# Second group's scores of layer 0 moved into the mixer stage, two gate spans of eight blocks, one-hot tiles with token pairs innermost

## The chip, the cores and the metric

One core of one Trainium2 chip runs the kernel. The time is device microseconds of one execution on that core; every value of the kernel is float32 unless a tile is marked F16. The profile names the engines PE (matrix products), PEld (their weight loads), DVE (vector), ACT (activation), POOL and SP.

## The reference

A step of a two-layer hybrid encoder, on 512 prompt rows (four blocks B0 to B3 of 128) and 64 sample rows (S), 1024 wide.

```
for each layer l in (0, 1):
    x += concat(DiffAttention, mLSTM, ChunkMLP)(rmsnorm(x) @ w_in) @ w_out     # the mixer
    q = rmsnorm(x) @ peer_wq                # 8 heads, two halves of 128 each
    s1, s2 = q_half @ keys.T                # 128 scores each; top 16 of each half
    e = top 16 of the 16 x 16 sums          # expert number: key1 * 128 + key2
    g = softmax of the 16 chosen sums       # per head
    h = gelu(u[e] . xn) * g                 # 8 x 16 = 128 experts a token, of 16384
    x += sum over e of h * v[e]             # the PEER step
y = rmsnorm(x)
```

The mixer's attention of a prompt block looks at its own and the earlier blocks, so B2 and B3 need B0 and B1 of the same layer, and not the other way round.

## The kernel before, in words

The tokens are in two groups, g1 = B0, B1, S and g2 = B2, B3. In each layer the groups pass a mixer stage and a PEER step. The mixer stage is made of parts: N (norm and transposes), P and Q (projections), M (mix), O (out projection), S (PEER queries, key scores and their top-16 selection, `scores` and `select_heads`), F (`finish_select`: expert numbers, softmax, and for dense blocks the transposed key numbers and gates in the tile `sel`). `ORDER` (L55) is the order of the parts by layer, written by hand; parts joined by "+" are woven, one step of each in turn (`weave`, L93). Each engine takes its instructions in an order that the scheduler builds at compile time from priorities, which are the program order; what `low` (L997) issues gets 10 million added and yields to everything else that is ready.

**PEER is done in two ways.** In each layer two blocks are dense: B0 and B1 in layer 0, B2 and B3 in layer 1. The others are sparse (S, B2, B3 in layer 0; S, B0, B1 in layer 1).

*Dense* (`peer_dense`, L1046): 128 chunks of 128 experts. `lead(c)` loads a U chunk (512 KB, queue of SP), does 8 matmuls into one half of the tile H (L1057) and a gelu on ACT into a tile A (L1066). Then A is multiplied by a slice of a gate block W on DVE (L1090), a V chunk (512 KB) is loaded, and 8 matmuls add to y (L1097). Leads run ahead of y by `LAG[l]` chunks; A has `LAG[l]` + 2 slots, and the first 8 x `PRE[l]` activations lie in gate blocks instead.

*Gate blocks.* W[experts of 8 chunks, 256 tokens] exist for 16 groups of 8 chunks. `gate_batch` (L1008) fills 8 tokens of several blocks at once: DVE compares the token's second key with 0 to 127 (o2, L1015), the first key with the block's own numbers (o1, L1016), and multiplies o1 by the gate's two F16 parts (L1018). PE makes 16 matmuls per batch (L1022), ACT copies the result into W (L1024). A span of blocks needs 32 batches. `QB` (L40) gives the spans: 4, 4 and 8 blocks. The first span is made in `first_gate` (L1033), the later ones in the last `WIN` chunks of the span ahead (L1079 to L1085). The tiles o2 and o1 have the 8 tokens innermost, so a matmul of one token steps over 8 F16 values, 16 bytes. `HOME` says in which pool a block lies: 0, "a" (beside the stream buffers) or "b" (`wb2`, memory that the selection's pool `sp` has until `close_scores`, L172; o1 lies there too, and in layer 0's first span in a spare block, "hot").

*Sparse* (`gather_u`, `gather_v`, L964 and L985): for each of 128 expert slots (64 for S) POOL gathers 128 rows of U by index (512 KB, L953) and DVE reduces them against the norm (L977); then the same with V, added to x (L989). All of it is issued by `low`. In layer 0 the first of it is held behind the last DVE operation of the first gate (`self.gated`, L973). B3's V rows of layer 0 run in layer 1's mixer, woven with M1 (`rest_v`, part R).

**Order around the change.** Layer 0's mixer stage ends with "S1+M2 F1 O2". `run` (L1147 to L1154) then does the norm of B0 and B1 for the dense stage, weaves `first_gate` with 2 leads, weaves 8 further leads with the scores of g2, finishes the selection of g2, and only then calls `close_scores`. In layer 1 the scores of g2 run in the dense stage too, ahead of `first_gate`, beside 24 leads.

Of the kernel before, what the change touches and what calls it, by code (L numbers as in the profile page):

```python
# [21 lines left out]
P = 128  # L22
# [17 lines left out]
QB = [[4, 4, 8], [4, 4, 8]]  # L40
WIN = [[14, 24], [16, 16]]
GATE_A, GATE_B = 4, [6, 5]
HOME = ["0aaaabbbbbb0aaaa", "0aabbbbbaa0aabbb"]
# [6 lines left out]
LAG = [2, 8]  # L50
PRE = [0, 2]
EARLY_LEADS = 5
LATE_LEADS = 8
REST_STEP, REST_PARTS = 4, 16
ORDER = ["N1 P1 N2 Q1 M1+P2 O1+Q2 S1+M2 F1 O2", "N1 P1 Q1 M1+R O1 S1 N2 P2 F1+Q2 M2 O2"]  # L55
# [65 lines left out]
class Build:  # L121
# [30 lines left out]
    def dense_pools(self, ec, l):  # L152
# [13 lines left out]
        self.whp, self.mixer = None, False  # L166
        ec = self.sel_es.enter_context
# [70 lines left out]
    def setup(self):  # L238
# [13 lines left out]
        self.jj = self.cp.tile([P, P, 8], F16, name="jj")  # L252

    def make_bias(self):
# [3 lines left out]
        nc.vector.tensor_copy(self.jj, iota[:, :, None].to_broadcast([P, P, 8]))  # L258
# [585 lines left out]
    def finish_select(self, l, g):  # L844
        nc = self.nc
        for t in sorted(g, key=lambda t: t.order):
# [34 lines left out]
            c0, c1 = t.c0, t.c0 + P  # L881
            for j in range(2):
                nc.scalar.activation(self.sel[:, j, c0:c1], pt[:, j, :], AF.Copy)
            gr = self.sp.tile([P, P], F32, tag="gr", name="gr")
            nc.scalar.activation(gr, pt[:, 2, :], AF.Copy, scale=GSCALE)
            nc.vector.tensor_copy(self.sel[:, 2, c0:c1], gr)
            nc.vector.tensor_tensor(self.sel[:, 3, c0:c1], gr, self.sel[:, 2, c0:c1], op=ALU.subtract)
# [36 lines left out]
    def lookup(self, t, h0, nh):  # L924
# [14 lines left out]
        for a in range(2):  # L939
            oh = self.sp.tile([P, TOPK, 16, PH], F16, tag="oh", name="oh")[:, :, :, :nh]  # L940
            nc.vector.tensor_tensor(oh, self.jj[:, None, :16, :nh].to_broadcast(sh),
# [55 lines left out]
    def low(self, fn, *a):  # L997
        p0 = self.tc.cur_priority
        self.tc.cur_priority = p0 + LOW
        fn(*a)  # L1000
        self.tc.cur_priority = p0
# [6 lines left out]
    def gate_batch(self, blocks, i0, t0, pb, hot=None):  # L1008
        nc, nq = self.nc, 8 * len(blocks)
        if hot is None:  # L1010
            o2 = self.d2.tile([P, P, 8], F16, tag="o2", name="o2")
            o1 = self.wb2.tile([P, 3, 64, 8], F16, tag="o1", name="o1", bufs=2)[:, :, :nq, :]
        else:
            o2, o1 = hot
        nc.vector.tensor_tensor(o2, self.jj, self.sel[:, 1, None, t0:t0 + 8].to_broadcast([P, P, 8]), op=ALU.is_equal)  # L1015
        nc.vector.tensor_tensor(o1[:, 2], self.jj[:, i0:i0 + nq, :], self.sel[:, 0, None, t0:t0 + 8].to_broadcast([P, nq, 8]),  # L1016
                                op=ALU.is_equal)
        self.mark = nc.vector.tensor_tensor(o1[:, 0:2], o1[:, 2:3].to_broadcast([P, 2, nq, 8]),  # L1018
                                            self.sel[:, 2:4, None, t0:t0 + 8].to_broadcast([P, 2, nq, 8]), op=ALU.mult)
        for j in range(8):  # L1020
            for p in range(2):
                nc.tensor.matmul(pb[:, j, :nq], o2[:, :, j], o1[:, p, :, j], start=(p == 0), stop=(p == 1))  # L1022
# [242 lines left out]
```

## Time and profile before

| what | value |
|---|---|
| median of 3 runs | 3736.93 us (3736.39 to 3742.16) |
| profiled execution, its own time | 3738.22 us |
| its span | 3736.5 us |
| granted TensorE clock, mean | 0.929 |
| busy: PE, DVE, POOL, ACT | 87%, 70%, 41%, 18% |
| bytes moved | 1060.34 MB, mean 284 GB/s |

Two lines of the page show the course of the work, in 40 equal slices of 93 us; the digits are tenths busy.

```profile
PE   8989879938999999998986796567678999999998
...
DVE  4554777898766666656068999879998767666641
```

Counted from 1, layer 0's mixer stage lasts into slice 6, its dense stage into slice 19, layer 1's mixer stage into slice 31, and the rest is its dense stage. A digit of 9 says that PE is the engine to look at there; where PE falls and DVE rises (slices 9, 25 to 30) it is DVE.

### The profile page before, as it was taken

To read this page: it belongs to the slowest core of one execution; us is meant where nothing else is said; L and a number is where in the kernel's file an instruction comes from. 1 tells how busy PE (TensorE), PEld (TensorE's weight loads), DVE (VectorE), ACT (ScalarE), POOL (GpSimd) and SP (SyncE) were. 2 spreads that over 40 slices of the span, in tenths; PEclk is the share of its full clock that TensorE was granted. 3 is DMA by queue.
4 is the path that set the end of the run, shared out by engine and by line. 5 is a ranking of instruction groups with operands and counts; after the bars stand their busy time and mean duration, and the time that the engine had idled before them with its cause. 6 is when DMAs were issued, how large, how long until landed. Compare 5 with 4: busy or idle time off the path is not lost.

```text
span 3736.5 us, 43654 instructions
## 1 busy us (share of the span) xinstructions
PE 3244.7 (87%) x14408; PEld 2238.5 (60%) x14408; DVE 2598.5 (70%) x6106; ACT 690.3 (18%) x2591; POOL 1531.7 (41%) x1284
## 2 busy tenths in 40 slices
PE   8989879938999999998986796567678999999998
PEld 6767657726777555554453554345565667766655
DVE  4554777898766666656068999879998767666641
ACT  5444232102121000001221222211121102100000
POOL 0000004455434655555036534655664553454420
PEclk9999988969999999999988898678888999999999
DMA  5332327978978999999368887989898898899973
GB/s 181 98 104 72 105 82 299 372 261 311 323 250 293 390 378 396 387 379 354 100 183 317 323 301 270 292 309 349 323 321 286 324 401 278 313 410 409 409 277 123
DMA packets 299937, 1060.34 MB, mean 284 GB/s; under 512 B 36372, under 2 KB 39232, under 8 KB 299712
## 3 DMA queue, kind: packets, MB, share of 16 engines
q0 software_dynamic: 184320, 671.17, 49.9%
q1 hardware_dynamic: 115392, 386.38, 28.1%
q8 instruction: 115, 1.88, 0.2%
q14 instruction: 110, 0.90, 0.1%
HBM read 1048.09 MB, written 8.27 MB: 283 GB/s over the span
## 4 chain that ended last, share of the span: by engine, by line
PE 61%; DVE 17%; DMA 13%; issue 5%; ACT 2%; POOL 1%; another core or an unknown queue 0%; SPq 0%; DVEq 0%; ACTq 0%; POOLq 0%
PE y L1097 19%; PE H L1057 18%; DMA row<-in_peer_v_dram,idx 8%; PE ps L392 7%; PE ps L403 5%; PE ps L1022 5%; DVE row L977 4%; DMA row<-in_peer_u_dram,idx 2%; DVE x_b L989 2%; PE ps L214 1%; POOL row L953 1%; DVE x_s L989 1%; DMA V<-in_peer_v_dram 1%; PE ps L568 1%; PE ps L570 1%
## 5 line engine op out<-in xcount | busy, mean ns | idle before, releaser
L953 POOL DMA_INDIRECT row<-in_peer_u_dram,idx x640 | 772.9, 1208 | 1331.2 <-DVE row L977 616.9
L953 POOL DMA_INDIRECT row<-in_peer_v_dram,idx x640 | 758.5, 1185 | 729.8 <-DVE x_b L989 475.2
L1097 PE MATMUL y<-V,A 128*128 128x512 f32 x1920 | 872.8, 598 | 12.5 <-DMA V<-in_peer_v_dram 12.5
L977 DVE SCALAR_TENSOR_TENSOR row<-row,xn 128x1024 f32<-128x1024 f32 x640 | 768.0, 1221 | 80.6 <-DMA row<-in_peer_u_dram,idx 74.5
L989 DVE SCALAR_TENSOR_TENSOR x_b<-row,hb,x_b 128x1024 f32<-128x1024 f32 x512 | 656.2, 1282 | 119.4 <-DMA row<-in_peer_v_dram,idx 106.8
L1097 PEld LDWEIGHTS y<-V,A 128*128 128x128 f32 x1920 | 365.3, 192 | 376.1 <-issue 361.7
L1057 PE MATMUL H<-xTd,U 128*128 128x256 f32 x2048 | 480.8, 388 | 37.7 <-ACT A L1066 35.5
L1057 PE MATMUL H<-xT,U 128*128 128x256 f32 x2048 | 478.6, 387 | 39.5 <-ACT pre L1066 19.7
L1057 PEld LDWEIGHTS H<-xTd,U 128*128 128x128 f32 x2048 | 385.2, 192 | 155.7 <-ACT A L1066 97.6
L1057 PEld LDWEIGHTS H<-xT,U 128*128 128x128 f32 x2048 | 393.7, 194 | 131.7 <-issue 55.4
L1090 DVE TENSOR_TENSOR A<-A,W 128x256 f32<-128x256 f32 x240 | 101.1, 423 | 393.2 <-ACT A L1066 385.5
L403 PE MATMUL ps<-xT,w 128*128 128x320 f32 (+1 forms) x1280 | 339.3, 420 | 25.0 <-DMA w<-in_wt_dram 16.2
L1066 ACT ACTIVATE A<-H 128x256 f32<-128x256 f32 x240 | 92.0, 384 | 1360.2 <-PE y L1097 677.4
L1022 PE MATMUL ps<-o,o 128*128 128x32 f16 (+1 forms) x2560 | 237.5, 264 | 102.7 <-DVE o L1018 102.7
L1022 PEld LDWEIGHTS <-o 128*128 128x128 f16 x2560 | 228.5, 151 | 143.6 <-DVE o L1018 104.5
L403 PEld LDWEIGHTS ps<-xT,w 128*128 128x128 f32 x1280 | 246.5, 196 | 96.1 <-DMA w<-in_wt_dram 16.6
L1024 ACT ACTIVATE W<-ps 128x64 f32<-128x64 f32 x1024 | 154.5, 307 | 386.9 <-PE ps L1022 363.1
L1015 DVE TENSOR_TENSOR o<-jj,sel 128x1024 f16<-128x1024 f16 x160 | 110.3, 690 | 108.5 <-PE ps L1022 104.9
L989 DVE SCALAR_TENSOR_TENSOR x_s<-row,hb,x_s 128x1024 f32<-128x1024 f32 x128 | 164.2, 1283 | 15.6 <-DMA row<-in_peer_v_dram,idx 14.1
L392 PE MATMUL ps<-w,xT 128*128 128x512 f32 (+3 forms) x320 | 127.1, 548 | 3.5 <-DMA w<-in_wn_dram 3.4
L347 DVE TENSOR_TENSOR wl<-w,wh 128x1024 fp32r<-128x1024 f32 (+1 forms) x56 | 64.4, 1149 | 75.3 <-PE ps L392 55.3
L392 PE MATMUL ps<-w,mix 128*128 128x512 f32 (+1 forms) x224 | 110.9, 648 | 5.5 <-DMA w<-in_wn_dram 3.9
(318 smaller groups left out, 3065.3 us busy)
## 6 DMA issues: line engine op xcount, KB each, us to landing
V<-in_peer_v_dram SPq DMA_DIRECT2D x256, 512.0 KB
U<-in_uT_dram SPq DMA_DIRECT2D x256, 512.0 KB
w<-in_wt_dram SPq DMA_DIRECT2D x96, 512.0 KB
w<-in_wn_dram SPq DMA_DIRECT2D x80, 512.0 KB
row<-in_peer_u_dram,idx POOLq DMA_INDIRECT x640
row<-in_peer_v_dram,idx POOLq DMA_INDIRECT x640
w<-in_keysT_dram SPq DMA_DIRECT2D x16, 256.0 KB
w<-in_wn_dram SPq DMA_DIRECT2D x8, 264.0 KB
```

Source lines behind the costliest of these rows:

```text
L392: self.nc.tensor.matmul(p[:t.n, :wd], x[kk][:, t.c0:t.c0 + t.n], ww[:, k * wd:(k + 1) * wd], start=(kk + part + j == 0), stop=(kk == KC - ...
L403: self.nc.tensor.matmul(ps, ww[:, k * P:(k + 1) * P], x[k][:, :n], start=(k + part + j == 0), stop=(k == KC - 1 and part == pair and j == ...
L953: self.nc.gpsimd.indirect_dma_start(out=row, out_offset=None, in_=self.h[tab], in_offset=bass.IndirectOffsetOnAxis(ap=t.idx[:, k:k + 1], a ...
L977: nc.vector.scalar_tensor_tensor(row, row, 1.0, xn, op0=ALU.mult, op1=ALU.mult, accum_out=hb[:, k:k + 1])
L989: op = nc.vector.scalar_tensor_tensor(x, row, t.hb[:, k:k + 1], x, op0=ALU.mult, op1=ALU.add)
L1015: nc.vector.tensor_tensor(o2, self.jj, self.sel[:, 1, None, t0:t0 + 8].to_broadcast([P, P, 8]), op=ALU.is_equal)
L1022: nc.tensor.matmul(pb[:, j, :nq], o2[:, :, j], o1[:, p, :, j], start=(p == 0), stop=(p == 1))
L1024: nc.scalar.activation(W[:, :, t0:t0 + 8].rearrange("p i t -> p t i"), pb[:, :, 8 * i:8 * i + 8], AF.Copy, scale=1.0 / GSCALE)
L1057: mm = nc.tensor.matmul(hp, U[:, k, :], xT[k], start=(k == 0), stop=(k == KC - 1))
L1066: nc.scalar.activation(a, hp, AF.Gelu)
L1090: gated = nc.vector.tensor_tensor(a, a, Ws[ci // 8][:, ci % 8, :], op=ALU.mult)
L1097: nc.tensor.matmul(ys[i][:, hf, :], a[:, i * P:(i + 1) * P], V[:, hf * 512:(hf + 1) * 512], start=(c == 0), stop=(c == NCH - 1))
```

## The change

The scores of g2 in layer 0 become a part of the mixer stage (S2, the last of its order), and their finish follows with a priority of its own (MID, ahead of the gathers, behind the rest). `close_scores` is called at once when layer 0's dense pools are opened. Both layers have two gate spans of 8 blocks; the second is made in the last 24 (layer 0) or 16 (layer 1) chunks of the first. Layer 0 takes 12 leads ahead (LAG 4, PRE 1) instead of 2, then 8 beside the scores. The one-hot tiles, the number table `jj` and `sel` are laid out with pairs of tokens innermost, so a matmul of one token steps over 2 F16 values, 4 bytes; the lookup of expert numbers gets a table of its own, `jl`.

```diff
@@ -37,22 +37,22 @@
 WT = 1056
 TD = 256
 NG = TD + NS
-QB = [[4, 4, 8], [4, 4, 8]]
-WIN = [[14, 24], [16, 16]]
+QB = [[8, 8], [8, 8]]
+WIN = [[24], [16]]
 GATE_A, GATE_B = 4, [6, 5]
-HOME = ["0aaaabbbbbb0aaaa", "0aabbbbbaa0aabbb"]
+HOME = ["0aaabbbbbba0aaab", "0aabbbbbaa0aabbb"]
+MID = 10 ** 6
 LOW = 10 ** 7
 PS_TAG = {"p": "mm", "a": "mm", "r": "mm", "o": "o", "tp": "tr", "ta": "tr", "tr": "tr"}
 PS_BUFS = {"mm": 4, "tr": 3, "o": 1}
 T_TAG = {"p": "t", "a": "t", "r": "tr"}
 T_BUFS = {"t": 4, "tr": 2}
 DENSE_T = 4
-LAG = [2, 8]
-PRE = [0, 2]
+LAG = [4, 8]
+PRE = [1, 2]
 EARLY_LEADS = 5
-LATE_LEADS = 8
 REST_STEP, REST_PARTS = 4, 16
-ORDER = ["N1 P1 N2 Q1 M1+P2 O1+Q2 S1+M2 F1 O2", "N1 P1 Q1 M1+R O1 S1 N2 P2 F1+Q2 M2 O2"]
+ORDER = ["N1 P1 N2 Q1 M1+P2 O1+Q2 S1+M2 F1+O2 S2", "N1 P1 Q1 M1+R O1 S1 N2 P2 F1+Q2 M2 O2"]
 NCH = NE // P
 
 C_ID, C_TRIU, C_MTS, C_MST, C_IOTA = [i * P for i in range(5)]
@@ -164,6 +164,8 @@
         self.ph = pool("ph", 1, space=PSUM)
         self.pm = pool("pmm2", 1, space=PSUM)
         self.whp, self.mixer = None, False
+        if l == 0:
+            return self.close_scores(ec, l)
         ec = self.sel_es.enter_context
         self.xg = pool("xg2", 1, side="right")
         self.t2 = pool("tmp2", DENSE_T, side="right")
@@ -249,13 +251,15 @@
         self.ident = cst[:, C_ID:C_ID + P]
         self.ones = self.cp.tile([P, 1], F32, name="ones")
         nc.vector.memset(self.ones, 1.0)
-        self.jj = self.cp.tile([P, P, 8], F16, name="jj")
+        self.jj = self.cp.tile([P, P, 2], F16, name="jj")
+        self.jl = self.cp.tile([P, 16, PH], F16, name="jl")
 
     def make_bias(self):
         nc, h = self.nc, self.h
         iota = self.tmp([P], "iota")
         nc.sync.dma_start(iota, h["consts"][:, C_IOTA:])
-        nc.vector.tensor_copy(self.jj, iota[:, :, None].to_broadcast([P, P, 8]))
+        nc.vector.tensor_copy(self.jj, iota[:, :, None].to_broadcast([P, P, 2]))
+        nc.vector.tensor_copy(self.jl, iota[:, :16, None].to_broadcast([P, 16, PH]))
         tab = self.sm.tile([32, NH], F32, name="tab", bufs=1)
         nc.sync.dma_start(tab, h["rel_table"])
         oh = self.tmp([N_OH + 1], "boh")
@@ -878,13 +882,16 @@
             f = "p k h -> p (k h)"
             for j, src in enumerate((es[:, 0].rearrange(f), es[:, 1].rearrange(f), gk)):
                 nc.tensor.transpose(pt[:, j, :], src, self.ident)
-            c0, c1 = t.c0, t.c0 + P
+            b0 = t.c0 // 8
+            sel = [self.sel[:, b0:b0 + 16, j, :] for j in range(4)]
+            f = "p (b c) -> p b c"
             for j in range(2):
-                nc.scalar.activation(self.sel[:, j, c0:c1], pt[:, j, :], AF.Copy)
+                nc.scalar.activation(sel[j], pt[:, j, :].rearrange(f, c=8), AF.Copy)
             gr = self.sp.tile([P, P], F32, tag="gr", name="gr")
             nc.scalar.activation(gr, pt[:, 2, :], AF.Copy, scale=GSCALE)
-            nc.vector.tensor_copy(self.sel[:, 2, c0:c1], gr)
-            nc.vector.tensor_tensor(self.sel[:, 3, c0:c1], gr, self.sel[:, 2, c0:c1], op=ALU.subtract)
+            gr = gr.rearrange(f, c=8)
+            nc.vector.tensor_copy(sel[2], gr)
+            nc.vector.tensor_tensor(sel[3], gr, sel[2], op=ALU.subtract)
             yield
 
     def make_idx(self, l, t, es, h0, nh):
@@ -938,7 +945,7 @@
         sh = [P, TOPK, 16, nh]
         for a in range(2):
             oh = self.sp.tile([P, TOPK, 16, PH], F16, tag="oh", name="oh")[:, :, :, :nh]
-            nc.vector.tensor_tensor(oh, self.jj[:, None, :16, :nh].to_broadcast(sh),
+            nc.vector.tensor_tensor(oh, self.jl[:, None, :, :nh].to_broadcast(sh),
                                     rc[:, a, :, None, :].to_broadcast(sh), op=ALU.is_equal)
             nc.vector.tensor_tensor(oh, oh, t.i16[:, a, None, :, h0:h0 + nh].to_broadcast(sh), op=ALU.mult)
             for m in (8, 4, 2):
@@ -994,9 +1001,9 @@
             nc.sync.dma_start(up[:NS], x[NS:P])
             nc.vector.tensor_tensor(x[:n], x[:n], up[:n], op=ALU.add)
 
-    def low(self, fn, *a):
+    def low(self, fn, *a, by=LOW):
         p0 = self.tc.cur_priority
-        self.tc.cur_priority = p0 + LOW
+        self.tc.cur_priority = p0 + by
         fn(*a)
         self.tc.cur_priority = p0
 
@@ -1005,21 +1012,20 @@
             self.low(self.gather_v, t, k, min(k + step, t.npair), self.last_dve())
             yield
 
-    def gate_batch(self, blocks, i0, t0, pb, hot=None):
+    def gate_batch(self, blocks, i0, t0, pb):
         nc, nq = self.nc, 8 * len(blocks)
-        if hot is None:
-            o2 = self.d2.tile([P, P, 8], F16, tag="o2", name="o2")
-            o1 = self.wb2.tile([P, 3, 64, 8], F16, tag="o1", name="o1", bufs=2)[:, :, :nq, :]
-        else:
-            o2, o1 = hot
-        nc.vector.tensor_tensor(o2, self.jj, self.sel[:, 1, None, t0:t0 + 8].to_broadcast([P, P, 8]), op=ALU.is_equal)
-        nc.vector.tensor_tensor(o1[:, 2], self.jj[:, i0:i0 + nq, :], self.sel[:, 0, None, t0:t0 + 8].to_broadcast([P, nq, 8]),
+        o2 = self.d2.tile([P, 4, P, 2], F16, tag="o2", name="o2")
+        o1 = self.wb2.tile([P, 3, 4, 64, 2], F16, tag="o1", name="o1", bufs=2)[:, :, :, :nq, :]
+        sel = self.sel[:, t0 // 8].rearrange("p r (c b) -> p r c b", b=2)
+        nc.vector.tensor_tensor(o2, self.jj[:, None].to_broadcast([P, 4, P, 2]), sel[:, 1, :, None, :].to_broadcast([P, 4, P, 2]),
                                 op=ALU.is_equal)
-        self.mark = nc.vector.tensor_tensor(o1[:, 0:2], o1[:, 2:3].to_broadcast([P, 2, nq, 8]),
-                                            self.sel[:, 2:4, None, t0:t0 + 8].to_broadcast([P, 2, nq, 8]), op=ALU.mult)
+        nc.vector.tensor_tensor(o1[:, 2], self.jj[:, None, i0:i0 + nq, :].to_broadcast([P, 4, nq, 2]),
+                                sel[:, 0, :, None, :].to_broadcast([P, 4, nq, 2]), op=ALU.is_equal)
+        self.mark = nc.vector.tensor_tensor(o1[:, 0:2], o1[:, 2:3].to_broadcast([P, 2, 4, nq, 2]),
+                                            sel[:, 2:4, :, None, :].to_broadcast([P, 2, 4, nq, 2]), op=ALU.mult)
         for j in range(8):
             for p in range(2):
-                nc.tensor.matmul(pb[:, j, :nq], o2[:, :, j], o1[:, p, :, j], start=(p == 0), stop=(p == 1))
+                nc.tensor.matmul(pb[:, j, :nq], o2[:, j // 2, :, j % 2], o1[:, p, j // 2, :, j % 2], start=(p == 0), stop=(p == 1))
         for i, W in enumerate(blocks):
             nc.scalar.activation(W[:, :, t0:t0 + 8].rearrange("p i t -> p t i"), pb[:, :, 8 * i:8 * i + 8], AF.Copy,
                                  scale=1.0 / GSCALE)
@@ -1032,14 +1038,9 @@
 
     def first_gate(self, l):
         nb = QB[l][0]
-        hots = None
-        if l == 0:
-            hot = self.wb.tile([P, 4 * P, 8], F16, tag="W", name="hot")
-            hots = [(hot[:, P * i:P * i + P], hot[:, 2 * P + 96 * i:2 * P + 96 * i + 96].rearrange("p (a i) t -> p a i t", a=3))
-                    for i in range(2)]
         self.W0 = [self.gate_block(l, i) for i in range(nb)]
         for t0 in range(0, TD, 8):
-            self.gate_batch(self.W0, 0, t0, self.psum([8, 8 * nb]), hots and hots[t0 // 8 % 2])
+            self.gate_batch(self.W0, 0, t0, self.psum([8, 8 * nb]))
             self.gated = self.mark
             yield
 
@@ -1126,7 +1127,7 @@
             D = g2 if l else g1[:2]
             for i, t in enumerate([S] + B):
                 t.dense, t.order, t.early = t in D, i, t.sample
-            self.sel = self.ca.tile([P, 4, TD], F16, tag="sel", name="sel")
+            self.sel = self.ca.tile([P, TD // 8, 4, 8], F16, tag="sel", name="sel")
             self.select_pool()
             with ExitStack() as es:
                 self.mixer_pools(es.enter_context, l)
@@ -1137,10 +1138,12 @@
                     "P2": lambda: [(self.project_a(l, L, g2), 4)], "Q2": lambda: [(self.project_b(l, L, g2), 2)],
                     "M1": lambda: self.mix(l, L, g1), "M2": lambda: self.mix(l, L, g2),
                     "O1": lambda: [(self.out_proj(l, g1), 2)], "O2": lambda: [(self.out_proj(l, g2), 2)],
-                    "S1": lambda: [(self.scores(l, L, g1), 18)], "F1": lambda: [(self.finish_select(l, g1), 3)],
+                    "S1": lambda: [(self.scores(l, L, g1), 18)], "S2": lambda: [(self.scores(l, L, g2), 18)], "F1": lambda: [(self.finish_select(l, g1), 3)],
                     "R": lambda: [(self.rest_v(B[3], REST_STEP), REST_PARTS)]}
                 for part in ORDER[l].split():
                     weave(*[s for k in part.split("+") for s in steps[k]()])
+                if l == 0:
+                    self.low(lambda: run(self.finish_select(l, g2)), by=MID)
             with ExitStack() as es:
                 self.dense_pools(es.enter_context, l)
                 nlead = LAG[l] + 8 * PRE[l]
@@ -1149,9 +1152,6 @@
                     self.norm_T(D, Q_G2, L, xT)
                     dense = self.peer_dense(l, D, xT)
                     weave((self.first_gate(l), 32), (itertools.islice(dense, nlead), nlead))
-                    weave((itertools.islice(dense, LATE_LEADS), LATE_LEADS), (self.scores(l, L, g2), 18))
-                    run(self.finish_select(l, g2))
-                    self.close_scores(es.enter_context, l)
                 else:
                     sc = self.scores(l, L, g2)
                     next(sc)
```

## Rows read from the trace of the kernel before

**Rows 1.** Windows of five stages: from:to, length, busy us and count, clock, DMA.

```profile
521.00:577.00 56.00, 52.52 (x599) 48.67 (x599) 37.28 (x91) 26.05 (x142) 0.00 (x0) 0.76 0.14 49
780.00:881.00 101.00, 32.52 (x210) 22.31 (x211) 92.32 (x211) 9.94 (x44) 51.92 (x39) 0.63 0.75 239
1768.00:1880.00 112.00, 105.80 (x326) 54.07 (x327) 17.00 (x47) 25.56 (x63) 9.54 (x8) 0.97 0.38 130
2197.00:2819.00 622.00, 414.00 (x1988) 304.37 (x1985) 562.72 (x1531) 114.03 (x397) 350.24 (x290) 0.82 0.89 314
3250.00:3600.00 350.00, 348.50 (x1210) 229.55 (x1210) 236.82 (x288) 21.31 (x55) 172.96 (x167) 1.00 1.02 406
```

**Rows 2.** Waits of PE, 575 to 900: engine, operation, for whom: total, times, longest.

```profile
PE ps L1022 <- DVE o L1018: 75.6, 2, 72.7
```

**Rows 3.** Timeline of PE, end of layer 0: start, us, operation, idle before.

```profile
1762.63 5.09 PE L1097 MATMUL y<-V,A 128*128 128x512 f32 x8 [3.32 <-DMA V<-in_peer_v_dram]
```

**Rows 4.** DVE gather rows by piece: ns min/median/max, first to last start.

```profile
L977 DVE SCALAR_TENSOR_TENSOR row<-row,xn x64: 1200/1222/1273, 579.5 to 712.6; 128x1024 f32<-128x1024 f32 x64
...
L977 DVE SCALAR_TENSOR_TENSOR row<-row,xn x128: 1210/1219/1293, 881.5 to 1216.8; 128x1024 f32<-128x1024 f32 x128
...
L989 DVE SCALAR_TENSOR_TENSOR x_b<-row,hb,x_b x128: 1276/1285/1311, 1218.0 to 1493.9; 128x1024 f32<-128x1024 f32 x128
...
L977 DVE SCALAR_TENSOR_TENSOR row<-row,xn x128: 1217/1220/1295, 1495.1 to 1764.3; 128x1024 f32<-128x1024 f32 x128
...
L989 DVE SCALAR_TENSOR_TENSOR x_b<-row,hb,x_b x128: 1227/1280/1310, 1863.6 to 2141.8; 128x1024 f32<-128x1024 f32 x128
```

**Rows 5.** Timeline of PE in layer 1: second group's transposes, P2, first y.

```profile
2166.96 1.95 PE L214 MATMUL ps<-dr,x_b 128*128 128x128 f32 x16
...
2197.11 3.27 PE L392 MATMUL ps<-w,xT 128*128 128x512 f32 x7
...
2819.11 9.37 PE L1097 MATMUL y<-V,pre 128*128 128x512 f32 x16 [1.32 <-DVE pre L1090]
```

**Rows 6.** Groups of DVE, 575 to 880, selection then finish, first and last of each.

```profile
L906 DVE FIND_INDEX8 i<-v,s 128x8 uint32<-128x128 f32 x32 | 8.9, 285 | 0.0
...
L945 DVE TENSOR_TENSOR oh<-oh 128x1024 f16<-128x1024 f16 (+2 forms) x12 | 5.5, 461 | 0.0
...
L906 DVE MATCH_VALUE_LOAD ci<-vsel,cand 128x8 f32 x16 | 1.2, 75 | 0.0
...
L854 DVE TENSOR_TENSOR ssg<-ssg 128x8 f32<-128x8 f32 x2 | 0.2, 156 | 0.0
```

**Rows 7.** Groups of PE, 575 to 880.

```profile
L403 PE MATMUL ps<-xT,w 128*128 128x256 f32 x256 | 58.9, 382 | 0.0
```

**Rows 8.** Timeline of PE: gate matmuls, 32 and 64 columns.

```profile
562.48 2.16 PE L1022 MATMUL ps<-hot 128*128 128x32 f16 x32 [0.37 <-DVE hot L1018]
565.01 2.15 PE L1022 MATMUL ps<-hot 128*128 128x32 f16 x32 [0.37 <-DVE hot L1018]
...
1041.32 3.98 PE L1022 MATMUL ps<-o,o 128*128 128x64 f16 x32
```

**Rows 9.** Groups of DVE by shape, whole span: the one-hot operations.

```profile
L1015 DVE TENSOR_TENSOR o<-jj,sel 128x1024 f16<-128x1024 f16 x160 | 110.3, 690 | 108.5 <-PE ps L1022 104.9 <-issue 2.7
...
L1018 DVE TENSOR_TENSOR o<-o,sel 128x1024 f16<-128x1024 f16 x64 | 43.2, 686 | 0.0
L1018 DVE TENSOR_TENSOR o<-o,sel 128x512 f16<-128x512 f16 x96 | 38.4, 421 | 0.1
...
L1016 DVE TENSOR_TENSOR o<-jj,sel 128x256 f16<-128x256 f16 x96 | 27.2, 285 | 0.0
```

**Rows 10.** Timeline of ACT: one gelu of each layer's dense stage.

```profile
1307.58 0.38 ACT L1066 ACTIVATE A<-H 128x256 f32<-128x256 f32 x1 [7.25 <-PE y L1097]
...
3451.03 0.38 ACT L1066 ACTIVATE A<-H 128x256 f32<-128x256 f32 x1 [6.50 <-issue]
```

**Rows 11.** Groups of DVE by shape: lookup with two heads innermost.

```profile
L941 DVE TENSOR_TENSOR oh<-jj,rc 128x512 f16<-128x512 f16 x8 | 4.9, 610 | 0.0
```

## The prediction

> **What bounds the kernel now.** I read five stages in the table of windows [rows 1] and asked of each what ends last. The first gate stage of layer 0 (521 to 577) keeps PE busy 52.5 of 56 us at a granted clock of 0.76, DVE 37.3. In 780 to 881 PE is busy only 32.5 of 101 us while DVE has 92.3: DVE selects experts for the second group and gathers, and PE stands 72.7 us on the one-hot tiles of the second gate span [rows 2]. So in layer 0 an early part of the dense stage is bound by DVE. The end of layer 0 looks different: the last y of the dense stage ends at 1767.7 [rows 3], and the next stage, layer 1's projections, leaves DVE idle (17 of 112 us) and DMA at 0.38 [rows 1].
>
> What joins the layers is the sparse chain, one row of U or V per token and expert slot, read by a POOL gather and consumed by DVE [rows 4]. It runs S, B2, B3, from 579.5 to 2143.1 (last start 2141.8 plus 1.28): 640 rows in 1564 us, 2.44 us each. By piece, each last row with 1.28: 2.10 (S u), 2.63 (B2 u, beside the gate spans), 2.16 (B2 v), 2.11 (B3 u), 2.18 (B3 v, in layer 1, tied behind its mixer and so begun 98 us after B3 u). B3's token block needs its last row before layer 1 can normalise the second group: its transposes end at 2168.9, 26 us after, and P2 starts at 2197.1, when the first group's scores leave PE [rows 5]. From there to the first y of layer 1 at 2819.1 [rows 5] DVE is busy 562.7 of 622 us [rows 1]: DVE bounds this stage. After it the dense stage of layer 1 takes the 918 us that are left, with PE at 348.5 of 350 us and DMA at 406 GB/s, its highest stage [rows 1]. The end is thus set by chain, then DVE, then PE.
>
> The sum is made against the profiled execution, 3738.2 us (span 3736.5); it lies 1.3 above the median of 3736.9. About 0.2%, or 7.5 us, is what a measurement of this kernel can tell from no change.
>
> **The change part by part.**
>
> *Scores of the second group into the mixer stage of layer 0.* Its DVE work moves ahead of the first gate. Selection: 18 rows from 8.9 to 1.2 us, together 79 us; finishing: 23 rows from 5.5 to 0.2, together 29 us [rows 6]. Its PE work is mainly 256 matmuls, 58.9 us in 16 steps [rows 7]; it issues 16 weight loads of 512 KB and 4 key loads of 256 KB (9.4 MB) on SP ahead of the U loads. At 406 GB/s that is 23 us that DMA has free here (share 0.14 [rows 1]), so I cost it at nothing; the cover is DVE's selection. DVE begins when the norm and the first four scores are there: four of the 16 steps (4 x 3.7, from 58.9 over 16 [rows 7]) and some 9 us of norm, 24 us. The finish has a priority behind the program and ahead of the gathers, but the memory of the second pool lies over the selection's, so one-hot tiles may wait for it; either way both stand before the first gather, which is held behind the last gate operation.
>
> *First gate of 8 blocks instead of 4.* Two 4-block batches start 2.52 us apart [rows 8], 1.26 each, where their DVE operations sum to 690 + 285 + 421 = 1396 ns [rows 9] one after the other. An 8-block batch is 690 + 421 + 686 = 1797; by the same ratio 1.62. 32 batches are 52 us instead of 40. So the first gate of layer 0 ends at 521 + 24 + 79 + 29 + 52 = 705; before, the chain began at 579.5, now at 709, 130 later. Without waiting for the finish the gate ends at 676, and the chain still begins at 705.
>
> *Dense stage of layer 0.* Twelve leads are done ahead, A has 6 slots instead of 4. Before, a gelu starts 0.38 + 7.25 = 7.63 us after the last, because it waits for y; in layer 1, with more slots, 6.88 [rows 10]. 116 leads at 6.88 are 798, the last 12 y, half a pitch each, 41, the one later gate span 34 (below), V waits at the end 7 (twice the 3.32 seen now [rows 3]): the end falls at 705 + 880 = 1585 (at 7.63: 1672), against 1768, so the first group's path is 96 to 183 us early. But it isn't what joins: the chain is.
>
> *The chain after.* It keeps its rows, loses the selection and one span beside it, and the gap of 98 us before B3 v, since the mixer it waits for comes early. S: 128 rows at 2.17, 709 to 989 (with 2 for norm). Then 20 to change tables and fold the sample. B2 u: 128 at 2.38 (between 2.16, all else gone, and 2.63, as now; one gate span of 58 us stands beside it where two stood), to 1314. B2 v at 2.16, 1590. B3 u at 2.0, since it now lies in layer 1's projections where DVE and DMA are free [rows 1], 1846. B3 v at 2.17, 2124. Plus 26, and some 8 for the crowded DVE: P2 starts at 2158 instead of 2197, **39 saved**. With all rows at 2.0 it is some 90; with B2 u at 2.63 and B3 u at 2.11, 46 later, it is nothing.
>
> *Layer 1 before its first y.* The first group arrives early, so its selection and finish lie beside the gathers instead of after P2's start. The most that this can take from the bound stage is a group's 79 + 29 = 108 [rows 6], the least nothing; it lies under a DVE already 90% busy, so nearer the low end: **30 saved**. Eight blocks instead of four: **11 more**.
>
> *Gate spans on PE.* Spans two and three cost 16 pairs of batches each, 2.15 us a pair at 32 columns and 3.98 at 64 [rows 8]: 34 + 64 = 98. Now one span of 64 columns. With pairs of tokens innermost, its operands step 4 bytes instead of 16. The added 32 columns cost 3.98 − 2.15 over 32, 57 ns each time. Bounds: 3.98 a pair if the step doesn't matter, half of 2.15 if it is all. The nearest row with 4-byte steps is a transpose: 16 matmuls of 128 columns in 1.95 us [rows 5], 122 ns each, so half as many columns about 61 to 67, 2.15 a pair: 34. So 64 off in layer 1, **60 saved**, since some turns into waits for V. [...]
>
> *One-hot operations on DVE.* I take them as unchanged, 690, 421 and 686 ns [rows 9]. The one row with two elements innermost says otherwise: 512 elements took 610 ns [rows 11] against 421; there the output also steps in rows of 16 bytes, which the new tiles don't, so I keep the old figure and make the row a rival. [...]
>
> *Sum.* 39 + 30 − 11 + 60 = 118: 3738.2 − 118 = 3620; the shift to the median is within the rounding. The bounds of the terms (0 to 90, 0 to 108, 30 to 64) give 3570 to 3670 when not all fall to one side.
>
> **The rivals.**
>
> *The chain keeps up* (0.14). If rows come at about 2.0 throughout, P2 starts some 90 early and the first group's selection lies wholly ahead: 3738 − 90 − 60 − 60 + 11 = 3540 (3505 to 3570). For: DVE loses a span and the selection beside it. Against: no stretch with dense work shows under 2.10 [rows 4].
>
> *The change doesn't do what it says on PE* (0.12). If the step doesn't matter, a pair stays at 3.98 and layer 1 loses 34 instead of 64: 3620 + 30 = 3650 (3620 to 3690). The layer 0 part is hidden by the chain.
>
> *DVE loses its rate on pairs* (0.12). A batch has 2560 elements, five times 512. At 610 − 421 = 189 ns more for each, 0.95 us a batch; at five times 610, 1.25: 31 to 40 us a span. Three spans stand on the path (layer 0's first, both of layer 1): 92 to 120 more, 3712 to 3740. For: the row of 610 ns.
>
> *Slower* (0.12). The chain starts 130 us later, at 709, and keeps its 2.44 us a row: 640 rows end at 2273, P2 starts at 2300, 103 later; with 11 and −30 and −60 it is 3738 + 24 = 3762 (3740 to 3790). Place: B2 u and v, which now lie beside a faster dense stage that asks DMA for 1 MB every 6.88 us instead of 7.63. It decides from 2.40 us a row, where the 78 us saved elsewhere are used up. Against: of 2.44, 0.15 is the gap of 98 us, and 0.09 the excess of B2 u over 2.16 beside gate spans of which one leaves.
>
> **How the numbers follow.** Forecast case 0.50, keeps up 0.14, step of no matter 0.12, rate lost 0.12, slower 0.12. I predict 3620. The range takes in keeping up and most of the lost rate, and leaves out the slow case and the far ends: 3530 to 3730. Faster by over 0.2%: 0.50 + 0.14 + 0.12 and a fifth of the lost rate, 0.78; within 0.2%: the upper half of the lost rate, 0.06; slower: 0.16.
>
> **What would show it.** Right: no stall of PE on one-hots in the middle of layer 0; first gather near 709; B2 u near 2.4 us a row; last row of B3 v near 2124; P2 near 2158; a pair of batches near 2.15 us on PE; one-hot operations at 690, 421 and 686. Wrong: gathers that begin much before or after 705, a chain at 2.44 a row, one-hot operations near 1.2 us, or a layer 1 whose stage before the first y is as long as before, although its start is early.

## The result and the profile after

The changed kernel takes 3611.1 us (median of 4 runs, 3604.3 to 3629.3) against 3738.8 for the kernel before (median of 4): a ratio of 0.9664 (0.9633 to 0.9695), 128 us less. The forecast was 3620. The profiled execution after is the slowest of its runs (3629.3, span 3627.6), so against its own counterpart it shows 109 us less; the lines below are to be read against that.

The table of windows, the stages that answer to [rows 1] (columns as there; the stage of 780 to 881 has no counterpart, so the stretch of B2's U rows stands in its place, and the last two lines cover layer 1's dense stage up to 3456):

```profile
615.00:724.00 109.00, 71.86 (x756) 63.15 (x754) 85.23 (x239) 41.85 (x281) 0.00 (x0) 0.83 0.26 75
1005.00:1340.00 335.00, 328.50 (x1407) 217.94 (x1407) 244.66 (x406) 40.65 (x211) 176.00 (x162) 1.00 1.01 393
1636.00:1790.00 154.00, 112.29 (x326) 55.78 (x326) 95.09 (x188) 26.67 (x65) 90.39 (x75) 0.84 0.86 315
2107.50:2746.40 638.90, 420.29 (x2002) 304.15 (x2001) 573.92 (x1526) 128.23 (x525) 364.40 (x289) 0.79 0.87 305
2746.40:3140.00 393.60, 365.86 (x1590) 224.42 (x1591) 303.15 (x454) 50.65 (x299) 251.80 (x192) 0.98 0.98 379
3140.00:3456.00 316.00, 305.58 (x1047) 196.90 (x1046) 213.07 (x245) 19.21 (x49) 185.45 (x147) 1.00 1.01 397
```

The first of these windows holds two things. Up to 649 DVE still selects, and PE waits for the one-hot tiles; then the first gate runs with the leads between its batches, and PE is what bounds it, at 59 of 59 us:

```profile
649.37 1.86 PE L1028 MATMUL ps<-o,o 128*128 128x64 f16 x32 [30.41 <-DVE o L1024]
```

```profile
658.00:717.00 59.00, 59.00 (x632) 52.27 (x631) 41.20 (x78) 31.42 (x221) 0.00 (x0) 1.00 0.40 117
```

So the 72.7 us for which PE stood in the middle of layer 0 [rows 2] are gone, but 30.4 us of such a wait now lie ahead of the first gate. Layer 1 before its first y is bound by DVE as before (574 of 639). Beside B2's U rows DMA is now as full as PE: share 1.01 with 393 GB/s (0.84 and 300 over B2's U rows before, 881 to 1219), PE busy 328.5 of 335 us. Right after layer 1's first y its share is 0.98, and PE is busy only 366 of 394 us. The sparse chain, DVE's rows by piece as in [rows 4]:

```profile
L984 DVE SCALAR_TENSOR_TENSOR row<-row,xn x64: 1207/1220/1289, 729.6 to 847.3; 128x1024 f32<-128x1024 f32 x64
...
L984 DVE SCALAR_TENSOR_TENSOR row<-row,xn x128: 1210/1225/1281, 1005.6 to 1266.3; 128x1024 f32<-128x1024 f32 x128
...
L996 DVE SCALAR_TENSOR_TENSOR x_b<-row,hb,x_b x128: 1277/1285/1289, 1269.0 to 1530.3; 128x1024 f32<-128x1024 f32 x128
...
L984 DVE SCALAR_TENSOR_TENSOR row<-row,xn x128: 1212/1225/1269, 1532.4 to 1792.0; 128x1024 f32<-128x1024 f32 x128
...
L996 DVE SCALAR_TENSOR_TENSOR x_b<-row,hb,x_b x128: 1234/1279/1339, 1796.1 to 2052.0; 128x1024 f32<-128x1024 f32 x128
```

It begins 150 us later and ends 90 earlier: 640 rows in 1324 us, 2.07 each instead of 2.44. B2's U rows went from 2.63 to 2.05, and the gap before B3's V rows from 98 us to 3. The timeline of PE, the ends of the stages as in [rows 3, 5, 8]:

```profile
667.44 1.12 PE L1028 MATMUL ps<-o,o 128*128 128x64 f16 x32
...
1632.64 3.67 PE L1098 MATMUL y<-V,A 128*128 128x512 f32 x8 [1.86 <-DMA V<-in_peer_v_dram]
...
2107.46 2.84 PE L396 MATMUL ps<-w,xT 128*128 128x512 f32 x6
...
2746.38 8.41 PE L1098 MATMUL y<-V,pre 128*128 128x512 f32 x16 [0.23 <-DVE pre L1091]
...
3604.89 7.03 PE L1098 MATMUL y<-V,A 128*128 128x512 f32 x16
```

A pair of 64-column batches takes 1.12 us (3.98 before). P2 starts at 2107.5 (90 earlier), the first y of layer 1 comes at 2746.4 (73 earlier), the last y ends at 3611.9. That end was at 3720.8 before:

```profile
3713.78 7.03 PE L1097 MATMUL y<-V,A 128*128 128x512 f32 x16
```

DVE's one-hot operations by shape, against [rows 9]. The last line is of the kernel before: its first span in layer 0 has a tile of its own, `hot`, which [rows 9] don't show.

```profile
L1020 DVE TENSOR_TENSOR o<-jj,sel 128x1024 f16<-128x1024 f16 x128 | 87.9, 688 | 41.2 <-PE ps L1028 39.8 <-remote 1.3
L1024 DVE TENSOR_TENSOR o<-o,sel 128x1024 f16<-128x1024 f16 x128 | 85.3, 685 | 0.0
L1022 DVE TENSOR_TENSOR o<-jj,sel 128x512 f16<-128x512 f16 x128 | 53.3, 417 | 0.0
```

```profile
L1015 DVE TENSOR_TENSOR hot<-jj,sel 128x1024 f16<-128x1024 f16 x32 | 22.0, 690 | 18.4 <-PE ps L1022 17.8
```

Their durations are the old ones. What changed is the column behind the bar: DVE's idle time ahead of a batch, put down to the gate matmuls. It was 104.9 us [rows 9] and 17.8 for `hot`, 122.7 over 192 batches, and is 39.8 over 128.

### The profile page after: what moved, and what is told of

The parts are those of the page before. It is cut to its first block, busy times and chain, and to the rows that moved or that the text cites. A ratio compares the mean times of both kernels' runs of the same rounds, so it can differ in the third digit from the quotient of the medians.

```text
span 3627.6 us, 41388 instructions
## 1 busy us (share of the span) xinstructions
PE 3095.5 (85%) x13384; PEld 2076.9 (57%) x13384; DVE 2563.4 (71%) x5915; ACT 670.5 (18%) x2589; POOL 1565.4 (43%) x1284
## 4 chain that ended last, share of the span: by engine, by line
PE 42%; DVE 17%; DMA 16%; issue 13%; POOL 7%; another core or an unknown queue 2%; ACT 2%; SPq 0%; POOLq 0%; DVEq 0%; ACTq 0%
PE y L1098 12%; PE H L1058 11%; DMA row<-in_peer_v_dram,idx 9%; POOL row L960 7%; PE ps L396 7%; PE ps L407 5%; DVE row L984 5%; DMA row<-in_peer_u_dram,idx 3%; DVE x_b L996 2%; DMA V<-in_peer_v_dram 2%; PE ps L572 1%; PE ps L1028 1%; PE ps L574 1%; DVE i L913 1%
## 5 line engine op out<-in xcount | busy, mean ns | idle before, releaser
L960 POOL DMA_INDIRECT row<-in_peer_v_dram,idx x640 | 792.0, 1238 | 522.4 <-DVE x_b L996 262.2
L1098 PE MATMUL y<-V,A 128*128 128x512 f32 x1856 | 835.1, 598 | 25.4 <-DMA V<-in_peer_v_dram 18.0
L1098 PEld LDWEIGHTS y<-V,A 128*128 128x128 f32 x1856 | 352.5, 192 | 403.0 <-issue 371.9
L1058 PE MATMUL H<-xTd,U 128*128 128x256 f32 x2048 | 470.1, 383 | 12.0 <-ACT A L1067 10.0
L1030 ACT ACTIVATE W<-ps 128x64 f32<-128x64 f32 x1024 | 137.5, 321 | 260.7 <-PE ps L1028 151.9
L1028 PE MATMUL ps<-o,o 128*128 128x64 f16 x2048 | 87.4, 200 | 73.9 <-DVE o L1024 73.7
L1028 PEld LDWEIGHTS <-o 128*128 128x128 f16 x2048 | 81.2, 103 | 106.5 <-issue 50.4
L1098 PE MATMUL y<-V,pre 128*128 128x512 f32 x192 | 100.6, 681 | 24.6 <-DMA V<-in_peer_v_dram 21.7
L1020 DVE TENSOR_TENSOR o<-jj,sel 128x1024 f16<-128x1024 f16 x128 | 87.9, 688 | 41.2 <-PE ps L1028 39.8
```

The costliest lines, as they stand in the source:

```text
L960: self.nc.gpsimd.indirect_dma_start(out=row, out_offset=None, in_=self.h[tab], in_offset=bass.IndirectOffsetOnAxis(ap=t.idx[:, k:k + 1], a ...
L1020: nc.vector.tensor_tensor(o2, self.jj[:, None].to_broadcast([P, 4, P, 2]), sel[:, 1, :, None, :].to_broadcast([P, 4, P, 2]), op=ALU.is_equal)
L1028: nc.tensor.matmul(pb[:, j, :nq], o2[:, j // 2, :, j % 2], o1[:, p, j // 2, :, j % 2], start=(p == 0), stop=(p == 1))
L1030: nc.scalar.activation(W[:, :, t0:t0 + 8].rearrange("p i t -> p t i"), pb[:, :, 8 * i:8 * i + 8], AF.Copy, scale=1.0 / GSCALE)
L1058: mm = nc.tensor.matmul(hp, U[:, k, :], xT[k], start=(k == 0), stop=(k == KC - 1))
L1098: nc.tensor.matmul(ys[i][:, hf, :], a[:, i * P:(i + 1) * P], V[:, hf * 512:(hf + 1) * 512], start=(c == 0), stop=(c == NCH - 1))
```

## The experiments

Ten runs take the change apart. In the table, ratios are to the kernel before on the same chip; the runs were spread over several chips, so rows are best compared by their ratios. The four times are those of each run's profiled execution: the first sparse row on DVE, the last B3 V row's end, the first y of layer 1, the end of the last y. Edits are shown in part, with `...` for what is left out.

| kernel | median us, ratio (interval) | first row | chain's end | first y, layer 1 | last y |
|---|---|---|---|---|---|
| before | | 579.5 | 2143.0 | 2819.1 | 3720.8 |
| changed | 3611.1, 0.9664 (0.9633 to 0.9695) | 729.6 | 2053.3 | 2746.4 | 3611.9 |
| changed, again | 3603.8, 0.9647 (0.9627 to 0.9666) | 737.6 | 2033.9 | 2727.9 | 3591.6 |
| before + early scores | 3700.1, 0.9908 (0.9881 to 0.9934) | 698.6 | 2086.6 | 2759.3 | 3680.8 |
| before + pairs | 3615.2, 0.9671 (0.9647 to 0.9696) | 569.3 | 2068.9 | 2746.6 | 3601.7 |
| changed, 16-byte steps | 3740.7, 1.0018 (1.0003 to 1.0032) | 779.8 | 2106.2 | 2805.3 | 3714.3 |
| before, half the gate matmuls | 3646.7, 0.9757 (0.9734 to 0.9780) | 571.5 | 2084.9 | 2743.4 | 3627.8 |
| changed, 4, 4, 8 in layer 1 | 3579.9, 0.9579 (0.9558 to 0.9601) | 725.5 | 2024.5 | 2694.9 | 3548.9 |
| changed, 4, 4, 8 in both | 3570.0, 0.9563 (0.9541 to 0.9585) | 720.0 | 2029.8 | 2695.0 | 3552.1 |
| the same, 2 leads | 3574.0, 0.9561 (0.9537 to 0.9584) | 691.0 | 2019.2 | 2688.7 | 3552.9 |
| changed, only o2 16-byte steps | 3650.7, 0.9754 (0.9730 to 0.9777) | 749.2 | 2078.8 | 2762.6 | 3640.0 |
| changed, only o1 16-byte steps | 3740.7, 1.0009 (0.9996 to 1.0022) | 782.5 | 2116.4 | 2817.7 | 3728.2 |

**The changed kernel again** (no edit).

> The changed kernel once more, timed in five rounds, and a second profile of it. Both theories expect 3605 to 3630 us and about 3.4% under the kernel before. If the profiled execution shows 3605 to 3612 instead of the 3629 of the first profile, the stage that differs between the two profiles is the one that scatters: I expect the stretch from P2 to the first y of layer 1 (639 us in the first profile) to be some 10 to 20 us shorter, since that is where DVE waits for gathers.

3603.8 us, 1 us under what was expected, and the stretch that differs is another: from P2 to the first y the second profile shows 640 us, no less than the first (639). It has the chain's end 19 us earlier, although the chain began 8 later; B3's U rows took 239 us instead of 261. Why they scatter was not tried.

**Early scores alone**, in the kernel before.

```diff
-"... S1+M2 F1 O2"
+"... S1+M2 F1+O2 S2"
...
+        if l == 0:
+            return self.close_scores(ec, l)
...
-        if l == 0:
+        if 0:
             hot = ...
...
+                if l == 0:
+                    self.low(lambda: run(self.finish_select(l, g2)), by=MID)
...
-                    weave((itertools.islice(dense, LATE_LEADS), LATE_LEADS), (self.scores(l, L, g2), 18))
-                    run(self.finish_select(l, g2))
-                    self.close_scores(es.enter_context, l)
```

The second pool opens early with it, and so the spare block `hot` is not needed.

> Kernel before with one part of the change: the second group's scores of layer 0 in the mixer stage, gate spans 4, 4, 8, old tiles and old leads. Theory 1 (moving the scores lets the sparse chain of layer 0 run at the rate of DMA): first gather near 715, 2.05 to 2.2 us a row all-in instead of 2.44, P2 at 2110 to 2150 instead of 2197, layer 1 from there as before, 3650 to 3690 us in all. Theory 2 (the chain gained from the shorter gate work on PE, and the move only exchanges places): 2.4 us a row, P2 near 2280 to 2300, 3800 us or more.

3700.1: 34 us saved, less than theory 1 had. The chain ends 56 us early, at 2.17 us a row, and P2 starts at 2141, both inside its bounds. Theory 2's figure (3800) is off, but so is theory 1's sum: the dense stage of layer 1, with the same code, took 20 us longer here (922 us instead of 902). The timeline of PE shows where, first the kernel before, then this one:

```profile
3703.44 3.62 PE L1057 MATMUL H<-xT,U 128*128 128x256 f32 x16
3706.90 3.60 PE L1097 MATMUL y<-V,A 128*128 128x512 f32 x8
3710.33 3.62 PE L1057 MATMUL H<-xT,U 128*128 128x256 f32 x16
```

```profile
3208.43 3.62 PE L1060 MATMUL H<-xT,U 128*128 128x256 f32 x16
3212.52 3.72 PE L1060 MATMUL H<-xT,U 128*128 128x256 f32 x16 [0.47 <-ACT A L1069]
3216.08 7.03 PE L1100 MATMUL y<-V,A 128*128 128x512 f32 x16
3222.95 3.62 PE L1060 MATMUL H<-xT,U 128*128 128x256 f32 x16
```

Before, PE takes one chunk's H and one chunk's y in turn, a chunk every 6.89 us. Here it takes two H and then two y, and the second H waits 0.47 us for a gelu: 14.52 us for two chunks, 0.74 more than twice 6.89. The wait comes 33 times; as an estimate from these figures that is 24 us. No edit asked for this order. It is the one that the scheduler built, and it also stands in the changed kernel and in the runs with 16-byte steps, half the gate matmuls and 2 leads, but not in "before + pairs" nor in the two runs with 4, 4, 8 and 12 leads. Those rows differ by it as well.

**Pairs alone**, in the kernel before.

```diff
-o2 = self.d2.tile([P, P, 8], F16, ...)
-o1 = self.wb2.tile([P, 3, 64, 8], F16, ...)[:, :, :nq, :]
+o2 = self.d2.tile([P, 4, P, 2], F16, ...)
+o1 = self.wb2.tile([P, 3, 4, 64, 2], F16, ...)[:, :, :, :nq, :]
...
-nc.tensor.matmul(pb[:, j, :nq], o2[:, :, j], o1[:, p, :, j], ...)
+nc.tensor.matmul(pb[:, j, :nq], o2[:, j // 2, :, j % 2], o1[:, p, j // 2, :, j % 2], ...)
```

> Kernel before with the other part alone: token pairs innermost in the one-hot tiles, all else as before. Theory 1: layer 0 up to P2 as before (2190 to 2205), the dense stage of layer 1 after its first y 30 to 50 us shorter than 902, 3690 to 3710 us in all. Theory 2: P2 is early too, by 50 to 90, and the whole at 3620 to 3660. Both expect a pair of batches of 64 columns near 1.12 us on PE (3.98 before) and one-hot operations at 690 and 421 ns.

3615.2, a little under theory 2's bounds. Here theory 1, which was the prediction's, falls: the layout alone gives nearly as much as the whole change (119 us), and 74 of its us come by the end of layer 0's chain, where I had put nothing; the chain begins 10 earlier and is 64 shorter. DVE's waits while B2's U rows run show how. First the kernel before (881 to 1219), then pairs alone (867 to 1148); the columns are waits of DVE, total us, times, longest:

```profile
DVE A L1090 <- ACT A L1066: 53.1, 20, 4.1
DVE o L1015 <- PE ps L1022: 38.8, 36, 3.0
DVE row L977 <- DMA row<-in_peer_u_dram,idx: 2.4, 4, 1.2
```

```profile
DVE A L1098 <- ACT A L1074: 33.6, 16, 3.8
DVE o L1021 <- PE ps L1029: 5.0, 6, 1.5
DVE row L982 <- DMA row<-in_peer_u_dram,idx: 4.7, 6, 2.4
```

In the order that the scheduler gave DVE, one-hot operations and gate products stand between the gathered rows. Before, the former waited 38.8 us for the tile that PE was still reading and the latter 53.1 for a gelu, while the rows behind them waited only 2.4 us for their own data: it was there when their turn came. That the gelu comes late because PE is at gate matmuls is the likely reading. The two waits fell from 91.9 to 38.6, by 53.3 us, and the 128 rows from 336.5 to 279.9, by 56.6.

**The old step in the changed kernel**: all 8 tokens innermost again, DVE still working on pairs.

```diff
-o2 = self.d2.tile([P, 4, P, 2], F16, ...)
+o2 = self.d2.tile([P, P, 4, 2], F16, ...)
-o1 = self.wb2.tile([P, 3, 4, 64, 2], F16, ...)[:, :, :, :nq, :]
+o1 = self.wb2.tile([P, 3, 64, 4, 2], F16, ...)[:, :, :nq]
...
```

> Changed kernel with the one-hot tiles laid out with all 8 tokens innermost again (matmul operands step 16 bytes, pairs still together for DVE). Theory 1: a pair of batches of 64 columns near 3.98 us on PE; the two first gates are paced by PE and 8 to 15 us longer each, P2 within 20 us of the changed kernel's, the dense stage of layer 1 after its first y 20 to 45 us longer; 3640 to 3690 us. Theory 2: the chain of layer 0 falls back to 2.3 us a row or more and the time to 3700 or more.

3740.7, no gain left: the chip's kernel before takes 3733.7, the changed kernel 3603.8 there. DVE's waits for gate matmuls are 161.5 us. Theory 2 had the time, but not the rate. B2's U rows take 2.24 us each instead of 2.05, yet the whole chain runs at 2.07 a row, not at 2.3 or more. Against the second profile of the changed kernel, the first sparse row comes 42 us later, since a pair of batches of the first gate now keeps PE for 3.98 us; the chain is 30 longer; and the dense stage of layer 1, where theory 1 had 20 to 45, is 45 longer.

**Half the gate matmuls**, in the kernel before, to tell PE's time from the layout. The kernel leaves out the second F16 part of a gate on PE.

```diff
-            for p in range(2):
-                nc.tensor.matmul(pb[:, j, :nq], o2[:, :, j], o1[:, p, :, j], start=(p == 0), stop=(p == 1))
+            nc.tensor.matmul(pb[:, j, :nq], o2[:, :, j], o1[:, 0, :, j], start=True, stop=True)
```

> Kernel before with its old tiles, but only the first of the two F16 parts of a gate is multiplied on PE (8 matmuls a batch instead of 16; the second part of the gate is left out of the result; DVE still makes it). It tells PE's time in a gate batch from everything else that the new layout changes. Theory 3 (DVE takes its instructions in order, so while it waits for PE's batches and for the gelu behind them, the gathers behind it wait too): a pair of 64-column batches near 2.0 us, DVE's waits for the gate matmuls 105 to some 40 us, B2's U rows 2.3 us each or less, last row of B3 v near 2080 to 2100, 3620 to 3660 us in all. [...]

3646.7, inside the bounds of theory 3: with old tiles and half of PE's gate time, 91 us are saved, where the pairs saved 119. The waits for the gate matmuls were 79.8 us with those of `hot` (122.7 before), 68.6 without (104.9), above the 40 that I expected; the rest of the figures nearly fit (B2's U rows 2.31, chain's end 2085). So it is PE's time in gate batches that counts. The two runs reach the first y of layer 1 together (2743 and 2747); the distance opens behind it, where this kernel has the order of two H and two y: 38 waits for gelus, by the same estimate 28 of the 29 us.

**Gate spans 4, 4, 8 with pairs**, in layer 1, in both layers, and in both with the old leads.

```diff
-QB = [[8, 8], [8, 8]]
+QB = [[8, 8], [4, 4, 8]]       # first run
+QB = [[4, 4, 8], [4, 4, 8]]    # second and third run
-LAG = [4, 8]
-PRE = [1, 2]
+LAG = [2, 8]                   # third run
+PRE = [0, 2]
```

> Changed kernel with gate spans 4, 4, 8 in layer 1 instead of 8, 8. Theory 3: layer 0 as in the changed kernel; the first gate of layer 1 is DVE work in a stage that DVE bounds, and 4 blocks need 11 to 16 us less of it; the further span then costs PE only some 13 us, hidden under DMA: from the last row of B3 v to the first y 677 us instead of 694, the rest 855 to 866; 3585 to 3595 us. Rival (the second later span's batches come back as DVE waits in the dense stage): 3605 to 3625 us.

> Changed kernel with gate spans 4, 4, 8 in both layers (scores early, 12 leads ahead, pairs innermost stay). Theory 3: first gather of layer 0 10 to 15 us earlier than in the changed kernel, but B2's U rows have two gate spans beside them again; chain's end within 15 us of the changed kernel's, layer 1 as in the run with 4, 4, 8 there; 3575 to 3600 us. Rival (three spans cost the chain): 3605 us or more.

> As the last run, but with 2 leads ahead in layer 0 as in the kernel before; against the kernel before with pairs alone (3615 us) it is the early scores alone. Theory 3: the dense stage of layer 0 waits for y again at a longer pitch, which leaves the chain more of DMA: chain's end within 15 us of the last run's, the same time within 15 us, so 3580 to 3610. Theory 1 (leads and A's slots matter): dense end 40 us or more later than with 12 leads and the whole 20 us or more slower.

3579.9, 3570.0 and 3574.0, each 5 to 6 us below theory 3's bounds. By the ratios, two spans of 8 in layer 1 cost the changed kernel some 25 us. From the chain's end to the first y they take 693 us, 4, 4, 8 takes 670 and 665. Behind the first y the two runs with 12 leads are 7 to 12 us shorter than the changed kernel although they have a span more; they have the order of one H and one y. The first gate stage on DVE, the kernel with 8 blocks (2647 to 2746), then that with 4 in layer 1 (2607 to 2695), groups as in [rows 9]:

```profile
L1024 DVE TENSOR_TENSOR o<-o,sel 128x1024 f16<-128x1024 f16 x33 | 22.0, 684 | 0.0
L1020 DVE TENSOR_TENSOR o<-jj,sel 128x1024 f16<-128x1024 f16 x32 | 21.9, 685 | 1.3 <-PE ps L1028 1.3
L1022 DVE TENSOR_TENSOR o<-jj,sel 128x512 f16<-128x512 f16 x33 | 13.8, 417 | 0.0
```

```profile
L1020 DVE TENSOR_TENSOR o<-jj,sel 128x1024 f16<-128x1024 f16 x32 | 22.0, 687 | 0.7 <-PE ps L1028 0.7
L1024 DVE TENSOR_TENSOR o<-o,sel 128x512 f16<-128x512 f16 x33 | 13.4, 415 | 0.0
L1022 DVE TENSOR_TENSOR o<-jj,sel 128x256 f16<-128x256 f16 x34 | 9.5, 281 | 0.0
```

13 us are these operations; where the other 10 to 15 before the first y go was not settled. The leads matter little: 12 ahead or 2 give the same time within the intervals, though the run with 2 has the order of two H and two y. The early scores are worth keeping: with pairs and 4, 4, 8, 2 leads, they are the only difference to "before + pairs", and 3615 becomes 3574 (ratio 0.9671, then 0.9561). The chain starts 122 us later and ends 50 earlier; 96 of these 172 are the gap before B3's V rows, 99 us there and 3 here: with the scores out of the way the dense stage of layer 0 ends earlier (its last y at 1629 instead of 1699), and layer 1's mixer, which these rows wait for, with it.

**Which operand's step**: first the stationary one (o2), then the moving one (o1) back at 16 bytes.

```diff
-o2 = self.d2.tile([P, 4, P, 2], F16, ...)             # first run
+o2 = self.d2.tile([P, P, 4, 2], F16, ...)
...
-o1 = self.wb2.tile([P, 3, 4, 64, 2], F16, ...)        # second run
+o1 = self.wb2.tile([P, 3, 64, 4, 2], F16, ...)
...
```

> Changed kernel with only the stationary operand (o2, the 128 columns that PE loads as weights) stepping 16 bytes again; the moving operand (o1) keeps 4 bytes. It tells which operand's step costs PE's time. If it is the moving one: a pair of 64-column batches stays near 1.1 to 1.3 us and the time within 15 us of the changed kernel, 3595 to 3620. If it is the stationary one: near 3.9 us a pair and 3720 to 3750 us. If both carry a part, between them. The old pairs took 2.15 us at 32 columns and 3.98 at 64, nearly in proportion to the moving columns, so I expect the moving one.

> The counterpart: only the moving operand (o1) steps 16 bytes again, the stationary one keeps 4. If the moving one costs the time: near 3.9 us a pair, DVE's waits for the gate matmuls near 160 us, 3720 to 3750 us in all. If the stationary one: 1.1 to 1.3 us a pair and 3595 to 3620 us.

The first run took 3650.7 us, by the ratios 34 to 40 more than the changed kernel and between the two cases; the second, 3740.7, came as expected for the moving operand. One pair of batches in the timeline of PE, for o2, then o1 at 16 bytes:

```profile
664.99 2.11 PE L1028 MATMUL ps<-o,o 128*128 128x64 f16 x32
```

```profile
666.63 3.87 PE L1028 MATMUL ps<-o,o 128*128 128x64 f16 x32
```

1.12 with both at 4, 2.11 with o2 at 16, 3.87 with o1, 3.98 with both: not a sum but nearly the larger of the two. By these figures the two costs overlap in time: the weights (o2) at 16 bytes make a pair 2.11 us long, the 64 moving columns (o1) 3.87. The old pair of 2.15 at 32 columns [rows 8] doesn't tell them apart, since half of 3.87 is 1.94. In both runs DVE's waits follow: 64.8 us and 158.8, against 39.8 with both at 4 bytes.

## Why the prediction was right, and where it was not

The number was right, but the working under it was not, and that it came out is luck: in the profiled executions the end of the chain gave 51 us more than its 39, layer 1 before its first y 36 less than its 19, the gate spans on PE 24 less than their 60, and these errors nearly cancel.

- *First sparse row at 709*: 729.6. The selection went as worked out (first gate matmul at 649). From there to the row it took 80 us, not 56, because the 12 leads are woven between the batches and PE paces them: a pair every 4.5 us (1.12 and a lead's 3.70, which overlap a little), where DVE's own pace would be 3.24 (twice the 1.62 of the forecast). With 2 leads and 4 blocks the row came at 691.
- *The chain after, 39 saved*: 90. It began 21 us late, was 91 shorter than worked out (1324 us instead of 1415), and P2 followed after 54 instead of 34. The failing step is the price of a row, "B2 u at 2.38" above all, with its cover "one gate span of 58 us stands beside it": I priced a span as DVE operations, and left out that DVE stands while PE reads. The number was in the rows, 104.9 us of idle time ahead of L1015 [rows 9]. B2's U rows took 2.05, 43 of the 91 us. With the old step they took 2.24, so 24 of the 43 us are that wait, and the other 19 are the estimate itself, too high even for the old step. S's rows and the V rows of B2 and B3 came at 2.00 to 2.05 instead of 2.16 to 2.17; they did so with the old step too (1.98 to 2.04), and no run shows why. That the gap of 98 us goes was right. The bound "with all rows at 2.0 it is some 90", from which the rival that the chain keeps up takes its price, is a wrong sum: 640 rows at 2.0 end at 2011 and save 152, and some 90 is what 2.1 a row gives.
- *"The layer 0 part is hidden by the chain"*, from the rival in which the step doesn't matter on PE: wrong for the same reason. It priced the loss at 30 us; undoing the step cost 137.
- *Dense stage of layer 0 ends at 1585 to 1672*: 1636.3.
- *Layer 1 before its first y, 30 saved and 11 more*: 17 more. The relief is not there: the stretch holds as many selection operations as before. The 8-block gate costs about twice its 11.
- *Gate spans on PE, 60 saved*: 36. A pair takes 1.12, not 2.15, so more PE time left than worked out (80 us, not 64). Of the 44 missing, some 26 are the order of two H and two y (35 waits at 0.74, an estimate), and waits for V grew from 8.8 to 21.6 us. They lie in the 394 us after the first y, where DMA is full (share 0.98 and 379 GB/s; before, 0.89 and 320 in the first 431); that DMA is the cause is not shown. The step does cost PE time: a pair of 64-column batches took 3.98 us with 16-byte steps and 1.12 with 4-byte ones.
- *One-hot operations unchanged*: 688, 417 and 685 ns with two tokens innermost, 690, 419 to 421 and 686 with eight. The rival of the lost rate is out. The lookup's 512 elements still take 609 ns; why was not tried.
- *Slower*: the chain did start 150 us late, but it ran at 2.07, far from its 2.40.

The best kernel of the study is the change without its two spans of 8: 4, 4, 8 in both layers, 3570.0 us, ratio 0.9563 (0.9541 to 0.9585), and with 2 leads the same within the intervals. No run has it with 2 leads and the order of one H and one y.

## What to carry to other kernels

Here the gate matmuls were paid on DVE as well: its one-hot operations waited 122.7 us for them in the kernel before and 39.8 in the changed one, and the gathered rows stood behind those waits. So a matmul's price has to be looked up on the engine that reuses its operands too: the column of idle time and its releaser says it before any change is made. And parts of a change are to be priced separately: here the pairs gave 119 us, the early scores 34 to 41, and the spans of 8 took some 25 back. Before two runs are compared by their times, look whether each engine takes its work in the same order in both; here an order that no edit asked for made a stage, by estimate, 24 to 28 us longer.

## What the runs showed of the hardware

A pair of batches has 32 matmuls. By its time over 32, a matmul of 64 moving F16 columns against 128 weights took 35 ns with both operands at steps of 4 bytes (1.12 us a pair, changed kernel), 66 with the weights at 16 (2.11), 121 with the moving columns at 16 (3.87) and 124 with both (3.98, before); at 32 columns it took 30 ns with both at 4 (0.95 us a pair, before + pairs) and 67 with both at 16 (2.15, before). I had expected 2.15 us a pair at 64 columns, not 1.12, and the cost in the moving operand alone.
